# A transformer block in split single precision: more weight pieces in seven products, more low parts by adding transfers

## The chip, the cores and the metric

One core of a Trainium2 chip runs the whole program. The metric is device time in microseconds (us), the median of the runs shown. The kernel before takes 2441.59 us (three runs, 2441.09 to 2441.65).

## The reference, cut to what matters

A block works on 256 tokens of 2048 features in float32: a feed-forward network (FFN), a mixer of two recurrences, cross attention, and a second FFN. The change is in the two FFNs, which have 5632 hidden features:

```python
def swiglu(h, w_up, w_down):
    gate, up = jnp.split(h @ w_up, 2, axis=-1)
    return (jax.nn.silu(gate) * up) @ w_down
...
x = x + 0.5 * swiglu(rms_norm(x, ffn1_norm[l]), ffn1_w_up[l], ffn1_w_down[l])
...
x = x + 0.5 * swiglu(rms_norm(x, ffn2_norm[l]), ffn2_w_up[l], ffn2_w_down[l])
```

`w_up` is 2048 x 11264 and `w_down` 5632 x 2048, so nearly all of an FFN is the streaming of weights through TensorE.

## The kernel before, in words

**Three matmuls for one product.** Every float32 operand is written as a sum of two parts in the type float32r: a high part `h` (the value rounded by ScalarE, line 120) and a low part `l` (value minus `h`, by VectorE, line 121). A product of two such operands is made of three matmuls, high by high, high by low, low by high; `three` (line 446) issues first the pairs that need only the weight's high part (lines 449 and 450), then the ones with its low part (line 452). One matmul here covers 128 x 128 activations by 128 x 512 weights.

**Pieces.** Weights come from DRAM as pieces of 128 x 2048 floats (1 MB). An FFN goes through 11 groups (512 gate columns and 512 up columns) of eight pieces each; piece p holds four blocks of 512 columns (a 2 x 2 arrangement) that meet the activations' pair p. A `plain` piece makes eight products, 24 matmuls. A `fast` piece makes the same contribution with seven products of sums and differences of blocks (the scheme known from Strassen and Winograd), 21 matmuls: VectorE first makes three blocks of differences `td` (lines 213 to 215), and both the three loaded blocks that are still used and the four-block tile of `td` with its copy are split into high and low: `h` and `l` (1536 columns) and `th` and `tl` (2 x 1024 columns, lines 217 to 221). A `mixed` piece makes eight products that add into the same sums as the seven do. `PRODUCTS` (line 458) lists them; in a fast piece the products with `h` and `l` come first (three of them), then the four with `th` and `tl`.

After the groups come `down` pieces (1 MB of `w_down`, 24 matmuls), four after each group from the fourth on, which take up the hidden features of two earlier groups. `turn` (line 483) turns a group's hidden features by transposes on TensorE.

**Order.** `ffn_order` (line 42) writes out the sequence. Before, groups 1 and 2 (counting from 0) have four mixed and four fast pieces; from group 3 on the order is pieces 1, 3, 0, 4, 2, 6, 5, 7 with 0 and 6 mixed. `weights` (line 165) prepares two pieces ahead; the order of instructions on the engines is otherwise set by the framework's scheduler when the program is built. On each engine instructions run in that order, each waiting for its semaphores.

**Low parts by transfers.** The mixed pieces from group 3 on have the kind `added`: `begin_added` (line 186) loads the piece, ScalarE writes `l = -raw`, and a DMA issued by GpSimd (line 192) adds the loaded piece to it, from on-chip memory to on-chip memory; ScalarE then writes `h` into another tile. Since adding into float32r leaves the difference from the rounded value, VectorE has no work on such a piece. `begin_added` is called one piece early.

**Buffers.** Three buffers each of the loaded piece (`raw`), of high parts (`h` and `th` share them), of low parts `l`, and of `wide` (`td`, `tl`, and the sums `ev` at the end of a group). A fast piece takes two of the three `h` buffers, so the `th` of a piece goes where the `h` of the piece before it stood, and can be written only when TensorE is through with that.

**Sums of activations.** A pair that meets fast pieces needs sums and differences of its blocks (`sums` in `operand_pairs`, line 424); a pair that meets mixed pieces needs differences `less` instead. Pairs in `BOTH` (line 403) need both, and keep `less` in an extra slot `xd`.

Of the kernel before, what the change touches and what calls it, by code (L numbers as in the profile page):

```python
# [10 lines left out]
ACT = mybir.ActivationFunctionType  # L11
ALU = mybir.AluOpType
# [7 lines left out]
NG = DFF // 512  # L20
# [21 lines left out]
def ffn_order():  # L42

    out, down = [("plain", 0, p) for p in range(8)], [("down", 0, 1, c, 0) for c in range(4)]
    for g in range(1, NG):
        if g < 3:  # L50
            out += [(("mixed", "fast")[p % 2], g, p) for p in (0, 1, 2, 3, 5, 4, 7, 6)]
        else:
            out += [("mixed" if p in (0, 6) else "fast", g, p) for p in (1, 3, 0, 4, 2, 6, 5, 7)]
        if g > 2 and g % 2:
            down = [("down", g - 2, 2, c, b) for c in range(4) for b in (g - 2, g - 1)]
        n = 2 if g < 3 else 4
        out, down = out + down[:n], down[n:]
    return out + [("down", NG - 2, 2, c, b) for c in range(4) for b in (NG - 2, NG - 1)]
# [3 lines left out]
def block_kernel(ctx: ExitStack, tc: tile.TileContext, xT, xin, memT, vec, gfin, bgate, lruw, wu1, wd1, win, wv,  # L62
                 wg, wab, wout, wq, wk, wvm, wo, wu2, wd2, out_):
    nc = tc.nc
    pe, dve, act, sp = nc.tensor, nc.vector, nc.scalar, nc.sync
# [21 lines left out]
    def slot(dt=F32, name="slot"):  # L87
        return slots.tile([P, 1024], dt, name=name, tag="slot")
# [12 lines left out]
    def col(name, i=0, n=1):  # L101
        a = VEC[name][0] + i
        return vt[:, a:a + n]
# [12 lines left out]
    done = {}  # L116


    def split(h, l, raw):
        done["high"] = act.activation(h, raw, ACT.Copy).ins  # L120
        done["low"] = dve.tensor_tensor(out=l, in0=raw, in1=h.bitcast(F32), op=ALU.subtract).ins  # L121

    def split_tiles():
        return hp.tile([P, 2048], F32R, name="h", tag="h"), lp.tile([P, 2048], F32R, name="l", tag="l")
# [5 lines left out]
    def plan_ffn(name, wu, wd):  # L130
        for e in orders[name]:
            src = wd[e[4], e[3]] if e[0] == "down" else wu[e[1], e[2]]
            kind = "fast" if e[0] == "fast" else "added" if e[0] == "mixed" and e[1] > 2 else "plain"
            plan.append(((name,) + e, src, kind))

    def plan_columns(name, w, which):
# [49 lines left out]
    def begin_added(src):  # L186

        raw = rawp.tile([P, 2048], F32, name="raw", tag="raw")
        l = lp.tile([P, 2048], F32R, name="l", tag="l")
        sp.dma_start(raw, src)  # L190
        act.activation(l, raw, ACT.Copy, scale=-1.0)
        nc.gpsimd.dma_start(l, raw, accum_op=ALU.add)
        return raw, l

    def prepare(src, kind, cuts=1):

        if kind == "added":
            raw, l = begun.pop(0)
            h = hp.tile([P, 2048], F32R, name="h", tag="h")
            done["high"] = act.activation(h, raw, ACT.Copy).ins  # L200
            return h, l
        raw = rawp.tile([P, 2048], F32, name="raw", tag="raw")
        n = 2048 // cuts
        if kind == "plain":
            h, l = split_tiles()
            for a in range(0, 2048, n):
                sp.dma_start(raw[:, a:a + n], src[:, a:a + n])
                split(h[:, a:a + n], l[:, a:a + n], raw[:, a:a + n])
            return h, l
        sp.dma_start(raw, src)  # L210
        td = scoped["wide"].tile([P, 2048], F32, name="td", tag="wide")
        two = [v[:, a:a + 1024].rearrange("p (i n) -> p i n", i=2) for v, a in ((td, 0), (raw, 512))]
        dve.tensor_tensor(out=two[0], in0=raw[:, None, :512].broadcast_to([P, 2, 512]), in1=two[1], op=ALU.subtract)
        dve.tensor_tensor(out=td[:, 1024:1536], in0=raw[:, 1024:1536], in1=td[:, :512], op=ALU.subtract)
        dve.tensor_tensor(out=td[:, 1536:], in0=raw[:, 1536:], in1=td[:, 1024:1536], op=ALU.subtract)
        h, l = split_tiles()
        split(h[:, 512:], l[:, 512:], raw[:, 512:])
        th = hp.tile([P, 2048], F32R, name="h", tag="h")
        tl = scoped["wide"].tile([P, 2048], F32R, name="tl", tag="wide")
        for a in (0, 1024):  # L220
            split(th[:, a:a + 1024], tl[:, a:a + 1024], td[:, a:a + 1024])
        return (h, l), (th, tl)
# [177 lines left out]

    BOTH = [2, 4]
    xd = []

    def operand_pairs(src, gain, q, xg, out):

        for a in src:
            i = len(out)
            g = xg[:, i * 512:(i + 1) * 512]  # L410
            for z in range(2):
                act.activation(g[:, z * T:][:, :T], a[:, z * T:(z + 1) * T], ACT.Copy,
                               scale=col(gain, 4 * q + 2 * i + z))
            h, l = slot(F32R, "xh"), slot(F32R, "xl")
            split(h[:, :512], l[:, :512], g)
            less = None if i else (h[:, 512:768], l[:, 512:768])
            if 2 * q + i in BOTH:
                if 2 * q + i == BOTH[0]:
                    xd.append(slot(F32R, "xd"))
                n = 512 * BOTH.index(2 * q + i)  # L420
                less = [xd[-1][:, a:a + 256] for a in (n, n + 256)]
            out.append(((h, l), less))

        def sums(which=((0, "less"), (0, "sums"), (1, "less"), (1, "sums"))):
            s = slot(name="xs")
            for i, ((h, l), less) in enumerate(out):
                a = [xg[:, i * 512 + j * P:][:, :P] for j in range(4)]

                def made(h, l, n, at, terms):
                    o = [s[:, at + j * P:][:, :P] for j in range(n)]  # L430
                    for j, (x, y, op) in enumerate(terms(o)):
                        dve.tensor_tensor(out=o[j], in0=x, in1=y, op=op)
                    split(h, l, s[:, at:at + n * P])

                if less and (i, "less") in which:
                    made(*less, 2, 0, lambda o: ((a[0], a[1], ALU.subtract), (a[2], a[3], ALU.subtract)))
                if (i or 2 * q in BOTH) and (i, "sums") in which:
                    if not i and len(which) > 1:
                        s = slot(name="xs")
                    made(h[:, 512:], l[:, 512:], 4, 512 * i,  # L440
                         lambda o: ((a[1], a[3], ALU.add), (o[0], a[0], ALU.subtract),
                                    (a[1], a[0], ALU.subtract), (a[2], o[1], ALU.subtract)))

        return sums
# [154 lines left out]
    def late_sums(q):  # L599
        with tc.issue_after(done["low"]):  # L600
            sums1[q](((0, "sums"),))

    for q, i in ((1, 16), (2, 17)):
        rest[i] = lambda q=q: late_sums(q)


# [580 lines left out]
```

## Time and profile before

| | |
|---|---|
| median of three runs | 2441.59 us |
| the profiled execution, its own time | 2441.09 us |
| its span, first to last instruction | 2439.3 us |
| outside the span | 1.8 us |
| first FFN, roughly | 0 to 670 us |
| second FFN, roughly | 1770 to 2430 us |
| one group from group 4 on (eight pieces and four down pieces) | 62.1 us |
| adding transfers | 32 |

The profile is one execution. PE is TensorE, DVE VectorE, ACT ScalarE, POOL GpSimd, SP the engine that issues the loads. A group of instructions is told by its line, its engine, its operation and `output<-inputs`. A matmul's own time (0.39 us) is longer than the distance between two starts, since they overlap; time on TensorE is therefore read from starts. The view in order of time has start, duration, engine, line, operation and, in brackets, idle time ahead of it with what ended it.

### The profile page before, as it was taken

The page shows a single profiled execution, that of the slowest core. Times are in us where ns is not written, and L with a number is a line of the kernel's source. Part 1 is how long each engine was busy: PE and PEld are TensorE (multiplying, and loading weights), DVE is VectorE, ACT ScalarE, POOL GpSimd, SP SyncE. Part 2 cuts the span into 40 slices and gives each one's busy share as a digit, 9 for nine tenths or more (in the row PEclk, how much of TensorE's full clock was granted, in tenths as well). Part 3 has the DMA queues.
Part 4 walks back from the last instruction along what each step waited for, and adds up shares of the span by engine and source line. Part 5 has one row for each costly group of instructions (what it writes and reads, how often), then busy time and mean ns, then how long its engine had stood idle before and what let it go on. Part 6 is the DMA issues. An engine that isn't in the chain of part 4 may idle for free.

```text
span 2439.3 us, 30196 instructions
## 1 busy us (share of the span) xinstructions
PE 2428.9 (100%) x12250; PEld 2034.0 (83%) x12250; DVE 1889.8 (77%) x2015; ACT 1394.5 (57%) x1399; POOL 28.1 (1%) x36
## 2 busy tenths in 40 slices
PE   9999999999999999999999999999999999999998
PEld 8888888888888888888888888888888888888887
DVE  7999999999865767577565676556589999999995
ACT  8566666666554454477435554455555666666664
POOL 0000000000000000000000000000000000000000
PEclk9999999999999999999999999999999999999999
DMA  7577767777655445445555555444555777777774
GB/s 293 194 224 258 250 233 236 234 238 237 214 188 190 173 173 182 173 172 216 194 186 190 209 192 188 172 172 156 190 190 187 249 238 233 234 238 242 237 234 150
DMA packets 75308, 509.69 MB, mean 209 GB/s; under 512 B 8352, under 2 KB 8608, under 8 KB 15264
## 3 DMA queue, kind: packets, MB, share of 16 engines
q1 hardware_dynamic: 69840, 473.06, 53.9%
q0 software_dynamic: 4608, 33.56, 6.8%
q8 instruction: 96, 1.57, 0.3%
q10 hardware_dynamic: 720, 1.13, 0.1%
q14 instruction: 44, 0.36, 0.0%
HBM read 472.07 MB, written 2.10 MB: 194 GB/s over the span
## 4 chain that ended last, share of the span: by engine, by line
PE 98%; DVE 1%; DMA 0%; ACT 0%; issue 0%; ACTq 0%; SPq 0%; DVEq 0%
PE acc L449 18%; PE acc L450 18%; PE acc L452 18%; PE acc L231 11%; PE acc L252 8%; PE acc L253 8%; PE acc L255 8%; PE acc L235 6%; PE acc L488 1%; PE acc L389 1%; DMA raw<-wu 0%; PE acc L764 0%; PE acc L1046 0%; PE acc L1001 0%; PE acc L867 0%; PE warm L109 0%
## 5 line engine op out<-in xcount | busy, mean ns | idle before, releaser
L121 DVE TENSOR_TENSOR l<-raw,h 128x2048 fp32r<-128x2048 f32 (+2 forms) x420 | 872.8, 2085 | 357.9 <-ACT h L120 346.1
L120 ACT ACTIVATE h<-raw 128x2048 fp32r<-128x2048 f32 (+2 forms) x420 | 732.8, 1752 | 626.2 <-PE acc L253 204.5
L449 PE MATMUL acc<-h,xh 128*128 128x512 f32 x1280 | 498.3, 390 | 0.4 <-ACT h L120 0.4
L450 PE MATMUL acc<-h,xl 128*128 128x512 f32 x1280 | 496.9, 389 | 0.0
L120 ACT ACTIVATE h<-td 128x1024 fp32r<-128x1024 f32 x224 | 229.2, 1055 | 180.1 <-PE acc L450 137.5
L252 PE MATMUL acc<-h,ops 128*128 128x512 f32 x832 | 326.9, 393 | 0.0
L253 PE MATMUL acc<-h,ops 128*128 128x512 f32 x832 | 324.3, 390 | 0.0
L121 DVE TENSOR_TENSOR tl<-td,h 128x1024 fp32r<-128x1024 f32 x224 | 267.0, 1220 | 32.3 <-ACT h L120 29.9
L449 PEld LDWEIGHTS acc<-h,xh 128*128 128x128 f32 x1280 | 240.3, 188 | 51.1 <-ACT h L120 1.1
L450 PEld LDWEIGHTS acc<-h,xl 128*128 128x128 f32 x1280 | 240.3, 188 | 49.5
L231 PE MATMUL acc<-ops,h 128*128 128x512 f32 x1152 | 278.0, 393 | 0.3
L449 PE MATMUL acc<-h,hidop 128*128 128x512 f32 x704 | 275.8, 392 | 0.0
L450 PE MATMUL acc<-h,hidop 128*128 128x512 f32 x704 | 274.3, 390 | 0.0
L231 PEld LDWEIGHTS acc<-ops,h 128*128 128x128 f32 x1152 | 211.9, 188 | 42.9 <-DVE ops L292 0.9
L452 PE MATMUL acc<-l,xh 128*128 128x512 f32 x832 | 218.6, 389 | 0.0
L255 PE MATMUL acc<-l,ops 128*128 128x512 f32 x832 | 206.1, 390 | 0.0
L452 PE MATMUL acc<-l,hidop 128*128 128x512 f32 x704 | 188.3, 389 | 0.0
L255 PEld LDWEIGHTS acc<-l,ops 128*128 128x128 f32 x832 | 156.2, 188 | 32.4
L252 PEld LDWEIGHTS acc<-h,ops 128*128 128x128 f32 x832 | 156.2, 188 | 32.3
L452 PEld LDWEIGHTS acc<-l,xh 128*128 128x128 f32 x832 | 156.1, 188 | 32.4
L253 PEld LDWEIGHTS acc<-h,ops 128*128 128x128 f32 x832 | 156.3, 188 | 31.6
L452 PEld LDWEIGHTS acc<-l,hidop 128*128 128x128 f32 x704 | 132.1, 188 | 27.5
(218 smaller groups left out, 2355.0 us busy)
## 6 DMA issues: line engine op xcount, KB each, us to landing
raw<-wu SPq DMA_DIRECT2D x172, 1024.0 KB, 4.9
raw<-wd SPq DMA_DIRECT2D x88, 1024.0 KB, 4.8
raw<-win SPq DMA_DIRECT2D x40, 1024.0 KB, 4.8
l<-raw POOLq DMA_DIRECT2D x32, 1024.0 KB, 7.3
raw<-wg SPq DMA_DIRECT2D x32, 1024.0 KB, 4.8
raw<-wab SPq DMA_DIRECT2D x16, 1024.0 KB, 4.8
raw<-wout SPq DMA_DIRECT2D x16, 1024.0 KB, 4.8
raw<-wq SPq DMA_DIRECT2D x16, 1024.0 KB, 4.8
```

The source lines that it names most:

```text
L120: done["high"] = act.activation(h, raw, ACT.Copy).ins
L121: done["low"] = dve.tensor_tensor(out=l, in0=raw, in1=h.bitcast(F32), op=ALU.subtract).ins
L231: pe.matmul(acc, h[:, k * P:(k + 1) * P], xs[k], start=k == 0, stop=False)
L235: done["product"] = pe.matmul(acc[:, :T], l[:, k * P:(k + 1) * P], xs[k][:, :T], start=False, stop=k == KT - 1).ins
L252: pe.matmul(accs[t], x[:, t * P:][:, :P], h[j], start=first and j == 0, stop=False)
L253: pe.matmul(accs[t], x[:, T + t * P:][:, :P], h[j], start=False, stop=False)
L255: done["product"] = pe.matmul(accs[t], x[:, t * P:][:, :P], l[j], start=False, stop=last and j == 3).ins
L389: pe.transpose(accs[m // 2][:, m % 2 * T + t * P:][:, :P], tile[:, t * 512 + m * P:][:, :P], ident)
L449: pe.matmul(acc, ah, bh, start=start, stop=False)
L450: pe.matmul(acc, al, bh, start=False, stop=False)
L452: pe.matmul(acc, ah, bl, start=False, stop=stop)
L488: pe.transpose(acc[:, z * T + t * P:][:, :P], hid[t][:, (2 * y + z) * P:][:, :P], ident)
```

## The change

From group 3 on the order becomes 1, 3, 4, 0, 2, 5, 6, 7 with only piece 0 mixed, so seven of eight pieces are fast. The kinds change with it. Mixed pieces become plain to prepare (VectorE makes their low part). Pieces 3, 4, 5 and 6 become `fast added`: as fast, but the low part of their three loaded blocks is made by ScalarE (`-raw`) and an adding transfer of 1536 columns. Down pieces of blocks 2, 4, 6 and 8 with an odd column c become `added` (8 per FFN). All adding transfers now read the piece from DRAM a second time, not the loaded tile. Pair 6 now needs both kinds of sums, which adds a second `xd` slot and one more late piece of sums in the first FFN.

```diff
         if g < 3:
             out += [(("mixed", "fast")[p % 2], g, p) for p in (0, 1, 2, 3, 5, 4, 7, 6)]
         else:
-            out += [("mixed" if p in (0, 6) else "fast", g, p) for p in (1, 3, 0, 4, 2, 6, 5, 7)]
+            out += [("fast" if p else "mixed", g, p) for p in (1, 3, 4, 0, 2, 5, 6, 7)]
...
-            kind = "fast" if e[0] == "fast" else "added" if e[0] == "mixed" and e[1] > 2 else "plain"
+            kind = "fast" if e[0] == "fast" else "plain"
+            if e[0] == "down" and 0 < e[4] < NG - 1 and e[4] % 2 == 0 and e[3] % 2:
+                kind = "added"
+            if e[0] == "fast" and e[1] > 2 and e[2] in (3, 4, 5, 6):
+                kind = "fast added"
...
-        nc.gpsimd.dma_start(l, raw, accum_op=ALU.add)
+        nc.gpsimd.dma_start(l, src, accum_op=ALU.add)
...
         h, l = split_tiles()
-        split(h[:, 512:], l[:, 512:], raw[:, 512:])
+        if kind == "fast":
+            split(h[:, 512:], l[:, 512:], raw[:, 512:])
+        else:
+            act.activation(l[:, 512:], raw[:, 512:], ACT.Copy, scale=-1.0)
+            nc.gpsimd.dma_start(l[:, 512:], src[:, 512:], accum_op=ALU.add)
+            done["high"] = act.activation(h[:, 512:], raw[:, 512:], ACT.Copy).ins
...
-    BOTH = [2, 4]
+    BOTH = [2, 4, 6]
...
-                if 2 * q + i == BOTH[0]:
+                n = 512 * (BOTH.index(2 * q + i) % 2)
+                if not n:
                     xd.append(slot(F32R, "xd"))
-                n = 512 * BOTH.index(2 * q + i)
...
-    for q, i in ((1, 16), (2, 17)):
+    for q, i in ((1, 16), (2, 17), (3, 18)):
         rest[i] = lambda q=q: late_sums(q)
```

## The prediction

> **What bounds the kernel now.** I read the page first (span, busy shares, chain that ended last), then what TensorE waited for, then one group of an FFN in order of time.
>
> ```profile
> span 2439.3 us, 30196 instructions
> PE 2428.9 (100%) x12250; PEld 2034.0 (83%) x12250; DVE 1889.8 (77%) x2015; ACT 1394.5 (57%) x1399; POOL 28.1 (1%) x36
> PE 98%; DVE 1%; DMA 0%; ACT 0%; issue 0%; ACTq 0%; SPq 0%; DVEq 0%
> PE acc L449 <- ACT h L120: 0.4, 1, 0.4
> ```
>
> The chain is 98% TensorE, and after the warm-up its only wait for another engine is 0.4 us. Nothing but fewer matmuls can shorten this, and there is no wait to remove. A busy PE could still be a slow one, so the stages and starts come next: one group in the windows view (columns: PE, PEld, DVE, ACT, POOL busy, granted clock, DMA share, GB/s), then starts on TensorE in one group.
>
> ```profile
> 400.00:462.10 62.10, 62.10 (x281) 51.51 (x279) 57.34 (x56) 38.37 (x32) 1.73 (x2) 1.00 0.73 237
> 100.00:160.00 60.00, 60.00 (x270) 49.57 (x269) 58.69 (x60) 32.56 (x27) 1.00 (x1) 1.00 0.61 211
> 1790.00:1850.00 60.00, 60.00 (x268) 49.31 (x268) 56.92 (x54) 32.16 (x26) 0.00 (x0) 1.00 0.57 200
> ```
>
> ```profile
> 368.29 0.39 PE L449 MATMUL acc<-h,xh 128*128 128x512 f32 x1
> ...
> 371.69 0.39 PE L450 MATMUL acc<-h,xl 128*128 128x512 f32 x1
> 371.91 1.98 PE L452 MATMUL acc<-l,xh 128*128 128x512 f32 x8
> 373.73 0.39 PE L449 MATMUL acc<-h,xh 128*128 128x512 f32 x1
> ...
> 378.49 0.39 PE L449 MATMUL acc<-h,xh 128*128 128x512 f32 x1
> ...
> 382.34 1.07 PE L452 MATMUL acc<-tl,xh 128*128 128x512 f32 x4
> 383.25 0.39 PE L449 MATMUL acc<-h,hidop 128*128 128x512 f32 x1
> ```
>
> The clock is full (1.00). Piece 6, mixed, runs from 368.29 to 373.73: 24 matmuls in 5.44 us, 0.2267 us each. Pieces 5 and 7, fast, take 4.76 us each, 21 times the same. VectorE is second: 57.34 of a group's 62.10 us, 4.8 us idle.
>
> **What the change removes.** Piece 6 of groups 3 to 10 becomes fast in both FFNs: 16 pieces lose 3 matmuls. In the order in which the programs' instructions stand, TensorE has 48 fewer, 16 each of lines 449, 450 and 452 of before. 48 x 0.2267 = 10.88 us. All of it lies on the chain. A group shrinks by 0.68 us to 61.42.
>
> **What it adds to the other engines, per group.** These rows of VectorE and ScalarE give prices (distances between starts, since neighbours overlap by 0.08 us).
>
> ```profile
> 330.55 2.28 DVE L121 TENSOR_TENSOR l<-raw,h 128x2048 fp32r<-128x2048 f32 x1
> 332.75 0.68 DVE L558 SCALAR_TENSOR_TENSOR x<-acc,x 128x512 f32<-128x512 f32 x1
> ...
> 349.15 1.22 DVE L213 TENSOR_TENSOR td<-raw 128x1024 f32<-128x1024 f32 x1
> 350.40 0.69 DVE L214 TENSOR_TENSOR td<-raw,td 128x512 f32<-128x512 f32 x1
> 351.13 0.69 DVE L215 TENSOR_TENSOR td<-raw,td 128x512 f32<-128x512 f32 x1
> 351.74 1.75 DVE L121 TENSOR_TENSOR l<-raw,h 128x1536 fp32r<-128x1536 f32 x1
> 353.41 2.35 DVE L121 TENSOR_TENSOR tl<-td,h 128x1024 fp32r<-128x1024 f32 x2
> 355.68 1.22 DVE L213 TENSOR_TENSOR td<-raw 128x1024 f32<-128x1024 f32 x1
> ...
> 376.43 2.36 DVE L121 TENSOR_TENSOR tl<-td,h 128x1024 fp32r<-128x1024 f32 x2 [0.98 <-ACT h L120]
> ```
>
> ```profile
> 372.16 1.49 ACT L120 ACTIVATE h<-raw 128x1536 fp32r<-128x1536 f32 x1 [3.20 <-PE acc L450]
> 375.33 2.01 ACT L120 ACTIVATE h<-td 128x1024 fp32r<-128x1024 f32 x2 [1.68 <-PE acc L450]
> 377.25 1.90 ACT L120 ACTIVATE h<-raw 128x2048 fp32r<-128x2048 f32 x1
> ```
>
> VectorE: one more set of `td` (1.25 + 0.73 + 0.61) and `tl` (2.27), 4.86; three fewer `l` of 1536 columns (six fast before, three of seven after), 3 x 1.67 = 5.01; one `l` of 2048 less for a down piece and one more for piece 0, 2.2 each. Sum -0.15 us: as busy as before, in a shorter group. ScalarE: six sets of `h` and `th` (1.4 + 1.9 each), two operations of 1.8 for each of two mixed pieces and one for each down piece made 34.2; seven sets, four negated copies of 1536 (1.4 each), one of 1.8 for piece 0, four for the down pieces and one negated copy make 39.5: 5.3 more on top of the 38.4 that the window shows, 44 of 61.4. Both engines have room on average; what matters is when.
>
> **The step that decides: piece 7.** Before, VectorE had no work in the two mixed pieces, a rest of two times 5.44 us. Its second half of piece 7's `tl` ended at 376.43 + 2.36 = 378.79, and TensorE wanted it two matmuls after 382.34: 4.0 us of lead. After, pieces 5 and 6 cost VectorE 2.59 + 2.27 = 4.86 us against TensorE's 4.76 and piece 7 costs 6.53, so the lead goes. I work it out from the last point where VectorE must wait for TensorE: `th` of piece 5 goes into the buffer of piece 2's `h`, free after the first 6 matmuls of piece 2. Above, ScalarE starts 0.25 us after a release (371.91 to 372.16); a negated copy just ahead of it costs 0.04 more. From the release:
> - 0.29, then 1.06 for half of `th`, 0.05 to VectorE: 1.40.
> - VectorE in the changed order: `tl` of 5 (2.27), `td` of 6 (2.59), 0.1 waiting for the second half of `th`, `tl` of 6 (2.27), first `td` of 7 (1.14), its `l` (1.67), second `td` (0.61), first half of `tl` (1.14), third `td` (0.61), then the `l` of the first down piece (2.20), which stands ahead of the second half of `tl` (1.22): 15.82. Done at 17.22.
> - TensorE wants it after the rest of piece 2 (15 matmuls), pieces 5 and 6 (42) and 19 of piece 7: 76 x 0.2267 = 17.23.
>
> The lead is 0.01 us: nil. Bounds of the stall: nothing, if any step is a little shorter; 1.1 us a group, if the 14 operations take full durations instead of overlapping by 0.08. The rows show overlap nearly throughout, so I take 0.1 us, 16 times: 1.6 us. Behind the waiting matmul stands the whole of TensorE, so a stall here is paid in full.
>
> **The transfers.** A new wait: `l` of pieces 3 to 6 needs copy, issue and landing.
>
> ```profile
> L192 POOL DMA_DIRECT2D l<-raw x32: 859/865/1002, 153.9 to 2337.2; - x32
> ...
> DMA to landing us min/median/max: 7.1/7.3/13.2
> ```
>
> ```profile
> raw<-wu SPq DMA_DIRECT2D x172, 1024.0 KB, 4.9
> ...
> q1 hardware_dynamic: 69840, 473.06, 53.9%
> q0 software_dynamic: 4608, 33.56, 6.8%
> ```
>
> The tightest is piece 4: its `l` takes the buffer of the last down piece, free as piece 1 begins; the copy stands behind an `h`, so 0.8 + 1.5 us later the transfer is issued, and TensorE wants it 9.52 + 14 x 0.2267 = 12.69 us in. It may take 10.3 us; piece 6 may take 10.7. No row shows an adding transfer from DRAM. Bounds: a plain load of 1 MB, 4.9; the slowest adding one, 13.2. I take under 7.3 (three quarters of the bytes): covered with 3 us to spare, so nothing. Load on the queues: by the shares, 1 MB costs 2.9 us of 16 engines as a load (0.539 x 2439 / 451 MB) and 5.2 us adding (0.068 x 2439 / 32); a group goes from 12 loads and 2 to 12 and an equivalent of 4, 56 of 61.4 us, 0.91 where the window says 0.73. Loads then land later: one that meets an adding transfer of 1536 columns (3.9) needs up to 8.8, and the same schedule issues loads 8 to 11 us ahead of their first use: nothing, or a part of a microsecond on an engine that still has a lead there.
>
> One rule speaks against five GpSimd transfers a group. VectorE's operations nearly all read two on-chip tiles, and the issue took 859 to 1002 ns throughout, beside a VectorE that was busy 57 of 62 us. The Trainium skill (SBUF — State Buffer, SBUF: two separate sides) says that VectorE's two-port operations lock GpSimd out of a shared port, so that its descriptors are late: 3.1 us where 0.62 was the time alone. By that, 2.5 us more would leave piece 4 a lead of 0.5 us, still no loss by itself. The narrow spread of the issues does not bear it out here.
>
> **The sums for pair 6.** Once in each FFN: four operations of 128 columns and one split.
>
> ```profile
> L432 DVE TENSOR_TENSOR xs<-xg 128x128 f32<-128x128 f32 x40 | 9.7, 282 | 0.0
> L121 DVE TENSOR_TENSOR xl<-xg,xh 128x512 fp32r<-128x512 f32 x16 | 11.0, 690 | 11.7 <-ACT xh L120 11.3
> ```
>
> 4 x 0.28 + 0.69 = 1.8 us of VectorE. In the first FFN they stand near 103 us, where VectorE has 1.31 us idle in 60: at least 0.5 and at most 1.8 shows on TensorE; I take 1.2. In the second FFN 3.1 us are idle: nothing, at most 1.8.
>
> **Sum.** Against the profiled execution's 2441.09 (2439.3 and 1.8 around it): - 10.88 + 1.6 + 1.2 = 2433.0. The median of the runs is 0.5 above: 2433.5 us.
>
> **The rivals.**
> 1. No stall at all: TensorE stays gapless and 48 matmuls go: 2430.7. For it: the leads of 3 to 4 us before; against: piece 7's is used up by the schedule above.
> 2. VectorE becomes the bound at piece 7, slower than before. With a stall s per group the time is 2431.9 + 16 s. For it: the schedule leaves nothing, and VectorE has 98% of its time taken at 100 to 160 us already. Against: 1.1 us needs every overlap lost. At s = 0.5 it gives 2439.9 (within 0.2% of before), at s = 1.1 2449.5; it decides from s = 0.6.
> 3. Low parts land late. With landing L a group loses (L - 10.3) + (L - 10.7): from 10.8 the gain is gone. At 13.2, the largest shown, 5.4 x 16 = 86 us: about 2520. For it: 0.91 of the engines taken, a DRAM source that no row shows. Against: 7.3 in all but a few.
>
> **How the numbers follow.** Small stalls as summed 0.52, with own range 2431 to 2437; none at all 0.19; VectorE's stall between 0.3 and 0.9 a group, within 0.2% of before, 0.13; over that 0.09; late landings 0.07. 0.2% is 4.9 us, about what a measurement of this kernel tells from no change. So faster 0.71, same 0.13, slower 0.16. The range goes from 2430, just under rival 1, to 2442, which takes in most of the middle case and leaves out slower ones.
>
> **What would show it.** In the changed profile: 48 fewer matmuls; starts of fast pieces 4.76 us apart, groups 61.4 to 61.6. A wait of TensorE on line 121's `tl` once a group, at piece 7, is the decisive step; a wait on `l` with the landing over 10 us is rival 3, a wait on ScalarE's `th` would mean that the negated copies stand in the way, which I count at nothing. The landing of the 1536-column transfers should read 5 to 7.3, DMA share about 0.9. The prediction is wrong if TensorE waits over 0.3 us in most groups, or if gaps at 100 to 160 us pass 2 us.

## The result, and the profile after

The changed kernel takes 2456.68 us (median of four runs, 2455.61 to 2457.71) against 2441.34 before: ratio 1.0063, 95% interval 1.0049 to 1.0077. It is slower by 15 us where 8 us less were forecast, and outside the range. Rival 3, low parts that land late, is what happened. Times below are medians; one of the ten runs of `load_later` took 3304.75 us at a granted clock of 0.686 and is left out of its median.

The page of the changed kernel, its span, busy shares and the chain that ended last:

```profile
span 2455.6 us, 30385 instructions
PE 2427.0 (99%) x12202; PEld 2025.3 (82%) x12202; DVE 1883.5 (77%) x2057; ACT 1486.4 (61%) x1481; POOL 70.1 (3%) x84
PE 88%; DMA 9%; ACT 1%; DVE 1%; issue 1%; ACTq 0%; SPq 0%; DVEq 0%
```

The 48 matmuls are gone (12250 to 12202) and VectorE's and ScalarE's shares are near what was worked out. New is 9% of the chain on DMA. What TensorE and its weight loads waited for (total us, times, longest):

```profile
PE acc L461 <- DMA l<-wu: 17.7, 19, 2.7
PE acc L458 <- ACT h L120: 0.8, 1, 0.8
...
PEld acc L461 <- DMA l<-wu: 26.7, 23, 3.2
PEld acc L461 <- DVE tl L121: 0.3, 1, 0.3
```

Nearly every wait is the first low-part matmul of a piece waiting for an adding transfer; VectorE's `tl`, the step called decisive, made 0.3 us. Read from the starts of matmuls in both FFNs, what the distances have over 0.2267 us adds up to 4.6 us before and 31.0 after, 23.7 of it at line 461 on `l`. 31.0 - 4.6 - 10.9 (the matmuls that went) = 15.5, against 2455.6 - 2439.3 = 16.3 in the spans: nearly the whole loss is stalls. Of the 23.7 us 15.4 stand at piece 6, fifteen stalls, one a group: in the last seven groups of the first FFN, and in all eight groups with transfers of the second. 3.8 more stand at pieces 5 and 6 of the first FFN's first group with transfers, the fourth group (group 3 in the code).

The adding transfers of the fast pieces, and the page's issues (median us to landing) and queues:

```profile
L225 POOL DMA_DIRECT2D l<-wu x64: 865/874/1007, 152.5 to 2362.8; - x64
...
DMA to landing us min/median/max: 6.8/9.7/12.8
```

```profile
q1 hardware_dynamic: 69840, 473.06, 52.5%
q0 software_dynamic: 11520, 67.11, 14.7%
...
raw<-wu SPq DMA_DIRECT2D x172, 1024.0 KB, 6.1
...
l<-wu POOLq DMA_DIRECT2D x64, 768.0 KB, 9.7
```

Three quarters of the bytes take 9.7 us where 1 MB took 7.3. Loads take 6.1 where they took 4.9. The issue on GpSimd stayed at 865 to 1007 ns.

One group (columns as in the prediction), then the end of piece 6 in the group before it, in order of time on TensorE:

```profile
411.60:473.20 61.60, 61.60 (x277) 50.82 (x276) 56.50 (x58) 44.26 (x36) 4.36 (x5) 1.00 0.91 270
```

```profile
383.77 0.39 PE L459 MATMUL acc<-h,xl 128*128 128x512 f32 x1
384.84 0.97 PE L461 MATMUL acc<-l,xh 128*128 128x512 f32 x3 [0.68 <-DMA l<-wu]
385.65 1.09 PE L461 MATMUL acc<-tl,xh 128*128 128x512 f32 x4
```

The group is as forecast (61.6 us, VectorE 56.5, ScalarE 44, DMA 0.91). Piece 6's low part was due at 384.0 and came 0.68 us later. Its transfer and the load next to it, by the rows of SP and POOL:

```profile
373.09 0.33 SPq L211 DMA_DIRECT2D raw<-wd  x1
...
373.40 0.89 POOL L225 DMA_DIRECT2D l<-wu  x1 [4.87 <-DVE td L219]
...
DMA to landing us min/median/max: 11.4/11.4/11.4
```

11.4 us from issue to landing, with 10.7 allowed by the prediction: 0.7 over, and the wait is 0.68 (0.84 by the starts). The allowance was nearly right; the landing wasn't. The same rows in the kernel before, for a piece 6 of its first FFN and a piece 6 at the start of the second:

```profile
415.61 0.33 SPq L210 DMA_DIRECT2D raw<-wu  x1
...
418.30 0.86 POOL L192 DMA_DIRECT2D l<-raw  x1 [15.26 <-ACT l L191]
...
DMA to landing us min/median/max: 7.2/7.2/7.2
...
1902.98 0.33 SPq L210 DMA_DIRECT2D raw<-wu  x1
...
1903.02 0.86 POOL L192 DMA_DIRECT2D l<-raw  x1 [16.65 <-ACT l L191]
...
DMA to landing us min/median/max: 13.2/13.2/13.2
```

Here a cause suggests itself, before any change: with a load issued 2.7 us ahead the transfer took 7.2 us, with one issued 0.04 us ahead 13.2. All three of the old kernel's 32 transfers with a load 0.7 us or less ahead took 11.0 to 13.2 us. After the change piece 6's transfer has a load about 0.3 us ahead of it in nearly every group (0.31 in the one shown). That is read off afterwards; the runs below had to show it.

### The profile page after: what moved, and what is told of

Same layout as the page of the kernel before. It is cut to its first block, busy times and chain, and to the rows that moved or that the text cites. A ratio compares the mean times of both kernels' runs of the same rounds, so it can differ in the third digit from the quotient of the medians.

```text
span 2455.6 us, 30385 instructions
## 1 busy us (share of the span) xinstructions
PE 2427.0 (99%) x12202; PEld 2025.3 (82%) x12202; DVE 1883.5 (77%) x2057; ACT 1486.4 (61%) x1481; POOL 70.1 (3%) x84
## 4 chain that ended last, share of the span: by engine, by line
PE 88%; DMA 9%; ACT 1%; DVE 1%; issue 1%; ACTq 0%; SPq 0%; DVEq 0%
PE acc L461 16%; PE acc L458 14%; PE acc L459 14%; PE acc L240 11%; DMA l<-wu 8%; PE acc L261 8%; PE acc L262 8%; PE acc L264 8%; PE acc L244 5%; ACT l L224 1%; PE acc L497 1%; DMA raw<-wu 1%; PE acc L398 1%; ACT h L120 0%; PE acc L773 0%
## 5 line engine op out<-in xcount | busy, mean ns | idle before, releaser
L121 DVE TENSOR_TENSOR l<-raw,h 128x2048 fp32r<-128x2048 f32 (+2 forms) x372 | 790.0, 2128 | 337.0 <-ACT h L120 335.4
L120 ACT ACTIVATE h<-raw 128x2048 fp32r<-128x2048 f32 (+2 forms) x372 | 662.0, 1784 | 471.3 <-PE acc L262 205.7
L458 PE MATMUL acc<-h,xh 128*128 128x512 f32 x1256 | 490.6, 391 | 0.8 <-ACT h L120 0.8
L459 PE MATMUL acc<-h,xl 128*128 128x512 f32 x1256 | 488.9, 390 | 0.0
L120 ACT ACTIVATE h<-td 128x1024 fp32r<-128x1024 f32 x256 | 266.0, 1057 | 180.2 <-PE acc L459 88.8
L121 DVE TENSOR_TENSOR tl<-td,h 128x1024 fp32r<-128x1024 f32 x256 | 308.5, 1221 | 68.5 <-ACT h L120 66.9
L461 PE MATMUL acc<-l,xh 128*128 128x512 f32 x744 | 202.6, 394 | 17.7 <-DMA l<-wu 17.7
L461 PEld LDWEIGHTS acc<-l,xh 128*128 128x128 f32 x744 | 138.2, 188 | 54.1 <-DMA l<-wu 26.7
L217 DVE TENSOR_TENSOR td<-raw 128x1024 f32<-128x1024 f32 x128 | 155.9, 1218 | 6.1 <-DMA raw<-wu 3.9
## 6 DMA issues: line engine op xcount, KB each, us to landing
l<-wd POOLq DMA_DIRECT2D x16, 1024.0 KB, 10.7
```

What stands on the lines that cost most here:

```text
L458: pe.matmul(acc, ah, bh, start=start, stop=False)
L459: pe.matmul(acc, al, bh, start=False, stop=False)
L461: pe.matmul(acc, ah, bl, start=False, stop=stop)
```

## The experiments

Ratios are to the kernel before, run beside it on the same chip, with a 95% interval. The theories: Q, two transfers issued close together hold each other up; S, the source in DRAM makes them slow; L (or D), the load on the DMA engines as a whole does; T, TensorE loses what the time to land exceeds the time allowed by; V, VectorE is late instead; and, later, N and H, what was issued just ahead of a transfer sets its landing (G: it doesn't). A first or last record is that of the transfer itself in the trace of DMA records, in us after its issue.

**Order of the pieces (spread).** The pieces with transfers are no longer neighbours.

```diff
-(1, 3, 4, 0, 2, 5, 6, 7)]
+(1, 3, 2, 4, 0, 5, 7, 6)]
```

> Only the order of the pieces of a group from group 3 on is changed, to 1, 3, 2, 4, 0, 5, 7, 6: the four pieces with adding transfers (3, 4, 5, 6) no longer come two in a row, and their number and bytes are the same. Theory Q (the changed kernel lost because two adding transfers and the loads between them come faster than the 16 DMA engines move them, so the second of two lands late): landing of the 768 KB transfers falls from a median of 9.7 us to about 8 or less, TensorE's waits on them from 44 us to under 10, time 2431 to 2438. Theory S (an adding transfer that reads DRAM is slow in itself): landing stays at 9 to 10 us and the time over 2445. Theory L (the load as a whole, 0.9 of the engines, is too much): landing stays over 9 us, waits on it spread over all four pieces, time over 2445.

2486.73 us, ratio 1.0187 [1.0172, 1.0202]. The waits of TensorE:

```profile
PE acc L458 <- ACT h L120: 20.6, 16, 2.4
PE acc L461 <- DMA l<-wu: 15.5, 14, 4.8
```

As the whole cause theory Q falls: the waits on `l` are nearly as long with the pairs apart, and waits on ScalarE's `h` come on top. Piece 4, now without a transfer or a load close by, has its first record at 1.6 us and lands in about 7. Pieces 5 and 6, with a load 0.7 to 2.1 us ahead or 0.24 us behind, still have first records at 2.6 to 4.9 us.

**The source (tile_source).** The transfers add the loaded tile, as before, not DRAM.

```diff
-            nc.gpsimd.dma_start(l[:, 512:], src[:, 512:], accum_op=ALU.add)
+            nc.gpsimd.dma_start(l[:, 512:], raw[:, 512:], accum_op=ALU.add)
```

(and the same in `begin_added`.)

> The changed kernel with every adding transfer reading the loaded tile on the chip, as before the change, in place of DRAM; the loaded tile is then held until the transfer has landed. Theory S: landing of the 768 KB transfers falls to 7 us or less, TensorE's waits on them go, time 2431 to 2438. Theory Q: the engines move the same bytes, so landing stays at 9 to 10 us and the loads come later as well: time 2450 to 2475.

2468.68 us, 1.0114 [1.0099, 1.0130].

```profile
l<-raw POOLq DMA_DIRECT2D x64, 768.0 KB, 8.1
```

```profile
PE acc L461 <- DMA l<-raw: 11.9, 9, 4.9
PE acc L458 <- ACT h L120: 11.3, 12, 2.2
```

The landing falls by 1.6 us and a third of the wait with it, but the tile is kept longer, loads come later, and waits on `h` take the place. The DRAM source is the better of the two, and a DMA record takes the same time from either (see the end): S is at most a part of the cause.

**Fewer transfers (one_of_pair, no_adding).** Fast pieces 3 and 5 only, then none at all (nor for down pieces).

```diff
-            if e[0] == "fast" and e[1] > 2 and e[2] in (3, 4, 5, 6):
+            if e[0] == "fast" and e[1] > 2 and e[2] in (3, 5):
```

> The changed kernel with adding transfers for pieces 3 and 5 alone; the low parts of 4 and 6 go back to VectorE. Theory Q: landing falls to 7 to 8 us and TensorE does not wait for it; VectorE has 3.3 us more in a group, about 60.5 of 61.4, and its lead at piece 7 is gone: 0.5 to 2 us a group on line 121's tiles, time 2440 to 2465. Theory S: half of the waits on the transfers remain, at both pieces that keep them.

> The changed kernel without any adding transfer: every low part by VectorE. 8.9 us more a group on VectorE, about 66 us of work for 61.4: VectorE becomes the bound, at 4.6 us or more a group, time 2505 to 2530 by every theory. If it is much less, the transfers were not needed.

one_of_pair 2449.71 us, 1.0037 [1.0023, 1.0051]; no_adding 2488.21 us, 1.0193 [1.0172, 1.0213]. Window 400 to 600 us, in that order:

```profile
400.00:600.00 200.00, 199.60 (x890) 162.99 (x889) 190.59 (x191) 132.30 (x111) 8.71 (x10) 1.00 0.80 245
```

```profile
400.00:600.00 200.00, 195.92 (x847) 154.23 (x846) 197.86 (x192) 114.10 (x96) 0.00 (x0) 1.00 0.55 198
```

Without transfers VectorE is the bound (197.86 of 200), so they are needed; no_adding cost less than expected. With two a group the landing was still 9.3 us, though the next adding transfer was at least 14 us away: theory Q expected 7 to 8. VectorE took two pieces more, and yet the kernel is 7.0 us faster than the changed one.

**Time to land against time allowed (tl_first, own_low, own_tl).** Three kernels give the late pieces more time: `tl`'s matmuls first; a fourth buffer for the `l` of pieces 4 and 6; both.

```diff
-        for acc, (ah, al), (bh, bl), _, stop in products:
+        n = 3 if len(products) == 7 else 0
+        for acc, (ah, al), (bh, bl), _, stop in products[n:] + products[:n]:
```

```diff
+        if kind == "fast own":
+            l = Later(scoped["low"].tile([P, 1536], F32R, name="l", tag="low"))
+        else:
+            l = lp.tile([P, 2048], F32R, name="l", tag="l")
```

> The changed kernel with one edit: a fast piece's seven low-part matmuls begin with the four on tl, and the three on l come last (piece order, transfers and loads stay). Theory T (each adding transfer lands as it does, 9 to 12 us after its issue, and the loss is only what it exceeds its time by): pieces 3, 4 and 6 get 4 x 0.2267 = 0.91 us more, piece 5 none, since its l buffer also comes free that much later. The stalls of the changed kernel in the first half (1.31, 1.08, 0.84, 0.07, 1.35, 1.14, 2.26 us at piece 6) shrink by 0.9 each, the stalls on l from 23.7 us to about 9, the time to 2440 to 2446; landing of the 768 KB transfers stays at 9 to 10 us in the median. Rival D (the DMA engines' load is what limits, and a stall only gives it time): the time stays above 2452 and waits on h or on l come back later in each group. Rival V (the late low part of tl was as near): waits of L461 on DVE tl of over 5 us appear.

> The changed kernel with a fourth buffer for low parts: pieces 4 and 6 of the groups from the fourth on keep their l in a tile of 1536 columns of its own, so that the negation of piece 6 needn't wait for piece 0's product. (For room, the scratch tile of the squares is bfloat16 in the ffn stages, and one ring of the small pool has two buffers, not three.) In the changed kernel that negation began at 371.50 us behind piece 0's product, while piece 6's raw tile was there by 369.35 us, so the transfer can be issued about 2 us earlier. Theory T: the stalls of 0.4 to 1.4 us at piece 6 go, 2436 to 2443 us. Rival A (an earlier issue only stands longer behind the transfer of piece 5 and the loads): first packets 5 to 6 us after the issue in place of 4, landing 11 to 13 us, and the time stays above 2450. Rival D (load as a whole): above 2452, with waits on h.

> Both edits at once: the four low matmuls on tl first, and the fourth buffer for the low parts of pieces 4 and 6. Theory T: no stall on l is left outside group 3; the time is that of before less most of the 10.88 us of the removed matmuls, 2431 to 2437. Rival D: within 3 us of the better of the two single edits or above 2445.

tl_first 2448.38 us, 1.0031 [1.0020, 1.0042]; own_low 2471.53, 1.0128 [1.0111, 1.0146]; own_tl 2473.71, 1.0135 [1.0117, 1.0153].

With `tl` first the landing stays at 9.8 us and the stalls on `l`, read from starts, fall from 23.7 to 10.2 us. That bears out T: what is lost is what the landing exceeds the allowance by. The time ended 2 us above the range expected. The fourth buffer failed for a reason not foreseen. ScalarE's negation of piece 6 then, in order of time:

```profile
377.82 1.49 ACT L235 ACTIVATE l<-raw 128x1536 fp32r<-128x1536 f32 x1 [0.58 <-DMA raw<-wu]
```

It no longer waits for a buffer but for its own load, which came late: in this group the transfer's issue is 6.9 us behind piece 5's, not 5.7, and the stalls at piece 6 are 1.2 to 3.3 us. None of the rivals named before says this. The median landing, 11.1 us, is in the range of rival A. Piece 4 shows one thing more. In most groups its transfer now goes out 1.4 us behind piece 3's with next to no load records between (3 at most). Its first record comes at 4.6 to 5.0 us, when piece 3's transfer is nearly through, and it lands in 11.9 to 13.4 us where it took 8.9 to 10.6. An adding transfer just ahead holds the next one up too, so theory Q is a part of the truth.

**Own size (half_low).** The transfers bring 1024 columns, VectorE subtracts 512.

```diff
-            act.activation(l[:, 512:], raw[:, 512:], ACT.Copy, scale=-1.0)
-            nc.gpsimd.dma_start(l[:, 512:], src[:, 512:], accum_op=ALU.add)
+            act.activation(l[:, 1024:], raw[:, 1024:], ACT.Copy, scale=-1.0)
+            nc.gpsimd.dma_start(l[:, 1024:], src[:, 1024:], accum_op=ALU.add)
+            split(h[:, 512:], l[:, 512:], raw[:, 512:])
...
```

The old line that makes all of `h` goes.

> The changed kernel, but the adding transfers of fast pieces bring only the last 1024 of the 1536 columns (512 KB, packets of 4096 B); VectorE subtracts the other 512 (about 0.68 us more a piece, 2.7 a group, where it has 4 to 5 us left of 62.6). It tells own size from what lies ahead: if the landing is mainly the transfer's own packets, it falls by a third, from 9.7 to about 6.5 us, and the waits on DMA l go, 2435 to 2445 us; if it is mainly what stands ahead of its first packet (4 us) and loads among its packets, landing falls by 1.7 us at the most (a third of the 5 us of its own), to 8 or more, and the time comes to 2440 to 2450. Either way VectorE's share in the window 400 to 600 us rises from 0.93 or so towards 0.97; if waits on DVE l or tl of over 10 us appear, VectorE has become the bound.

2526.60 us, 1.0348 [1.0332, 1.0365].

```profile
PE acc L458 <- ACT h L120: 28.2, 25, 4.1
PE acc L461 <- DVE tl L121: 9.7, 13, 2.6
PE acc L461 <- DVE l L121: 6.8, 4, 4.5
```

No wait on a transfer is left and the landing is 6.5 us, but with 0.68 us more of VectorE ahead of each `tl` the waits move to `h`, `tl` and `l` made by the engines. The run says little of the landing, since stalls space the transfers out; it says how little lead VectorE has.

**The DMA engines' load (down_plain).** The down pieces' transfers, 18 to 20 us away from the others, go.

```diff
-                kind = "added"
+                kind = "plain"
```

> The changed kernel without the adding transfers of the down pieces (one down piece in four): VectorE makes those 16 low parts again, 2.29 us each, one a group. The transfer that goes was issued at 393.66 us, 20 us after piece 6's (373.39) and 18 us before the next piece 3's (411.76). Theory N (what lies just ahead in the queues sets the landing): the first packets stay at +1.6 us for pieces 3 and at +4 us or more for the others, the median landing stays between 9.3 and 10, and piece 6 waits as before; the waits of the low weight loads on DMA l stay at 20 to 27 us. Theory L (the DMA engines' share of the whole stage sets it): the share in 400 to 600 us falls from 0.90 to about 0.85 and the landing with it to 8.5 to 9, the waits to half. Time by N 2454 to 2465 (VectorE's 2.29 us a group cost little or some), by L 2445 to 2452.

2459.77 us, 1.0074 [1.0059, 1.0089]. The window, and the waits:

```profile
400.00:600.00 200.00, 198.29 (x887) 163.26 (x886) 187.14 (x186) 133.39 (x111) 10.45 (x12) 1.00 0.78 247
```

```profile
PE acc L461 <- DMA l<-wu: 17.9, 20, 3.2
```

DMA share 0.90 to 0.78, landing 9.8 (piece 6's last record at 10.97 us, 11.04 in the changed kernel), waits 17.9 against 17.7: the share of the stage isn't the cause, and N holds but for a detail. In most groups piece 3's first record came at 4.6 to 4.9 us and not at 1.6, where a load now went out 0.14 us behind its issue: a load just behind gets ahead as well.

**Transfers elsewhere (three_tl, early, early_fa).** With `tl` first: no transfer for piece 6; transfers for piece 0 and two down pieces in four, begun a piece early, and for no fast piece; for piece 0, pieces 3 and 4 and one down piece in four. The first edit is three_tl's; the second is in early and early_fa, which also limit the fast pieces and the down pieces as said.

```diff
-            if e[0] == "fast" and e[1] > 2 and e[2] in (3, 4, 5, 6):
+            if e[0] == "fast" and e[1] > 2 and e[2] in (3, 4, 5):
```

```diff
-            kind = "fast" if e[0] == "fast" else "plain"
+            kind = "fast" if e[0] == "fast" else "added" if e[0] == "mixed" and e[1] > 2 else "plain"
```

> The kernel with tl's low matmuls first, and no adding transfer for piece 6 (VectorE subtracts its 1536 columns again, 1.75 us a group). In the kernel with tl first the stalls left on l over 0.3 us are 8, seven of them at piece 6 or in the fourth group, 8.1 us together. Theory N: with that transfer out, piece 5's is the last of its group and lands in 9 to 10.5 us, no stall on l over 0.5 us is left after the fourth group, and the time is 2436 to 2444. Theory L agrees in the sign but expects landing of all of them to fall by the share (0.90 to 0.85). Rival V: VectorE at 0.94 of the stage makes pieces late and the time stays at 2447 to 2453, with waits on ScalarE's h and DVE's tl in place of DMA l.

> The seven products of the changed kernel with tl's low matmuls first, but the adding transfers where the kernel before had its kind: piece 0 whole, its load, negation and transfer begun a piece ahead, and two of the four down pieces, begun a piece ahead as well; no fast piece has one. So 3 MB of adding transfers a group against 2 before and 4 in the changed kernel. Theory T (time to land decides): landing of the 1 MB transfers 9 to 11 us, none late, waits on DMA l under 3 us; VectorE does all 1536-column low parts of the fast pieces, 7 us a group more than in the changed kernel less 4.6, so it stands at about 0.95 of the stage; 2432 to 2442 if that is enough, over 2445 with waits on h and tl if it isn't (rival V, as where only pieces 3 and 5 had transfers, 2449.7).

> Tl's low matmuls first; adding transfers for piece 0 whole (begun a piece ahead), for fast pieces 3 and 4, and for one down piece in four: 3.5 MB a group. Pieces 5 and 6, where the changed kernel waited, have VectorE's low parts. Piece 0's load and transfer now stand between piece 3's and piece 4's, so piece 4 has what piece 6 had: theory N expects first packets of +4 us or more and late low parts there, 2440 to 2450; theory L (share about 0.87) 2440 or less, with no place that waits above the others. VectorE's share is 0.92 to 0.94.

three_tl 2460.64 us, 1.0079 [1.0064, 1.0094]; early 2580.69, 1.0572 [1.0556, 1.0587]; early_fa 2588.43, 1.0601 [1.0584, 1.0619]. One row each, in that order:

```profile
PE acc L462 <- DVE tl L121: 11.8, 7, 3.9
```

```profile
PE acc L462 <- DMA l<-wd: 99.6, 18, 7.4
```

```profile
PE acc L462 <- DMA l<-wu: 104.2, 16, 9.1
```

In three_tl piece 6's 1.75 us put back on VectorE cost more than its late transfer (rival V). The other two were far worse than expected, and T's small waits for early were wrong: in the transfer records most of its transfers stand 0.4 to 1.8 us behind a load and the down pieces' land 11.6 us after issue, and in early_fa piece 4's stands behind piece 0's, 4.7 us ahead, and among loads, with first records at +4.3 to +7.3 us and last ones at +11 to +16.

**What stands ahead.** Read record by record, medians of the groups after the first with transfers, first FFN (us after the issue; a 1 MB load has 128 records; the last column counts records of loads that start while the transfer's own run):

```
kernel, piece        first record   last record   load records among
before, 0                1.63           6.97              1
before, 6                1.49           6.98             15
changed, 3               1.59           6.70             27
changed, 4               3.98           8.92             44
changed, 5               3.69           9.16             89
changed, 6               4.14          11.04            165
one_of_pair, 5           4.64           9.41             43
own_low, 4               4.83          11.77            137
```

Piece 3's transfer, with the last load ahead issued 5.7 us before it in most groups, is as fast as those before. Two things can stand ahead of a transfer. One is a load: in one_of_pair one goes out within 0.05 us of piece 5's transfer, and 117 to 129 records of loads run between that issue and the transfer's first record, in both FFNs. Piece 4 of the changed kernel, with its load 1.7 us ahead, has 115 to 128 in most groups. The other is an adding transfer still under way, as in own_low at piece 4. Piece 6 of the changed kernel has both: piece 5's transfer, whose last record comes 3.2 to 4.8 us after piece 6's issue, and the load 0.31 us ahead, whose records run partly ahead of piece 6's own (133 load records in the group shown, 24 to 58 in nine others) and partly among them. load_later moves this one load, the first down piece's: a write of one column, queued on ScalarE behind piece 6's `h`, keeps it back.

```diff
+            if e[0] == "down" and plan[-1][0][1:2] == ("fast",) and plan[-1][0][2] > 2:
+                kind = "plain later"
...
+        if kind == "plain later":
+            with tc.issue_after(done["six"]):
+                act.activation(raw[:, :1], ones[:, :1], ACT.Copy)
+            kind = "plain"
...
-            done["high"] = act.activation(h[:, 512:], raw[:, 512:], ACT.Copy).ins
+            done["high"] = done["six"] = act.activation(h[:, 512:], raw[:, 512:], ACT.Copy).ins
```

> The changed kernel with one load moved: the load of the first down piece of a group, which SP issued 0.30 us before piece 6's adding transfer (373.09 against 373.39 us), waits for a write of one column by ScalarE behind piece 6's h, so that it goes out some 3 us after the transfer. Theory H (a transfer's first packet waits for the packets of a load issued in the 2 us before it; with the load 2.4 us or more ahead, as in the kernel before, or none, the first packet comes at +1.5): first packets of piece 6's transfers at +1.5 to +2.5 us in place of +4.0 to +4.4, its landing 7 to 9.5 us, and its 15 stalls, 15.4 us together, go: 2440 to 2446 us. The down piece's load comes 3.3 us later and lands at about 382, its h was made at 384.25; if that is too tight, waits on ScalarE's h of 2 us or less a group appear. Rival G (the packets of the adding transfer are slow themselves or stand behind what all queues hold): first packets stay at +4 and more, the stalls stay, 2455 to 2470.

2444.66 us, 1.0016 [1.0007, 1.0026]: 12.0 us of the 15.3 come back with one load a group issued 3.3 us later. SP, POOL and landing of the same group, then window and waits:

```profile
371.66 0.89 POOL L231 DMA_DIRECT2D l<-wu  x1 [4.58 <-DVE td L225]
...
374.68 0.33 SPq L217 DMA_DIRECT2D raw<-wd  x1
...
DMA to landing us min/median/max: 9.1/9.1/9.1
```

```profile
400.00:600.00 200.00, 200.00 (x899) 165.50 (x899) 181.07 (x186) 141.67 (x122) 14.80 (x17) 1.00 0.90 273
```

```profile
PE acc L467 <- DMA l<-wu: 4.7, 4, 2.8
```

Landing 11.4 to 9.1, TensorE busy throughout in 400 to 600 us at the same DMA share of 0.90, and of the fifteen stalls at piece 6 one of 0.25 us is left. Instead `tl` of piece 7 is now late once a group, by 0.06 to 0.36 us, 2.4 us in all. One detail was wrong: first records come at 3.60 us, not 1.5 to 2.5, since piece 5's transfer is still ahead (its last record at +4.05 in this group). So most of the gain isn't at the start of the transfer: the load's records come after the transfer's and no longer among them (last record 11.04 to 8.11, load records among 165 to 44).

**What is left (load_later_tl, load_later_g4, later_g3_34, later_g3_345, later_g4).** On top of the load moved: `tl` first; that and no transfers for fast pieces in the fourth group; and, with `tl` in its old place, no transfers in that group for pieces 5 and 6, for piece 6, or for all four.

```diff
-            if e[0] == "fast" and e[1] > 2 and e[2] in (3, 4, 5, 6):
+            if e[0] == "fast" and e[1] > 2 and e[2] in (3, 4, 5, 6) and (e[1] > 3 or e[2] < 5):
```

(later_g3_34; `e[2] < 6` in later_g3_345, `e[1] > 3` alone in the two g4.)

> The load moved and tl's low matmuls first, both: by theory H with 0.91 us more for pieces 3, 4 and 6 what is left of waits on DMA l is the fourth group's (2 us) and piece 4's, under 4 us in all; 2434 to 2442 us. Rival G: as with tl's low matmuls first alone, 2447 to 2455.

> As the last, and fast pieces have adding transfers only from the fifth group on: the fourth group, where stalls of 0.88 and 2.90 us stood in the changed kernel in the first half, has VectorE's low parts. By theory H with the low parts' place in the start of the transfers: 1 to 4 us less than the last, 2432 to 2440. Rival V: VectorE's 7 us more in that one group make it late in both halves, and the time is 2 to 8 us over the last.

> The kernel with the load moved (tl's matmuls in their first place), and in the fourth group, the first with adding transfers, only pieces 3 and 4 have them. With the load moved, stalls of 0.68 and 3.00 us were left at pieces 5 and 6 of that group (186.91 and 193.91 us). Theory H with the start of the transfers as its last weak place: these go and VectorE's 3.5 us are covered: 2440 to 2443 us, no faster than before. Rival V: VectorE falls behind and the waits move to tl or h, 2445 to 2452 us.

> As the last, but only piece 6 of the fourth group is without an adding transfer: VectorE has 1.75 us more there. The stall of 3.00 us goes and the 0.68 may stay: 2440.5 to 2443.5 us by theory H, 2445 to 2450 by rival V.

> As the load moved, and adding transfers of fast pieces only from the fifth group on. With tl's matmuls first this gave 2458.8 us, with waits on DVE tl of 17 us. If it was tl's earlier place that made these, the time comes to 2440 to 2447 here; if it was VectorE's 7 us more in the fourth group, it stays above 2450.

In this order: 2450.32 us, 1.0039 [1.0024, 1.0054]; 2458.77, 1.0071 [1.0055, 1.0088]; 2452.62, 1.0049 [1.0036, 1.0063]; 2449.99, 1.0034 [1.0021, 1.0047]; 2454.21, 1.0055 [1.0043, 1.0068]. A row of TensorE's waits in load_later_tl:

```profile
PE acc L468 <- DVE tl L121: 5.8, 8, 3.1
```

All go to rival V. load_later_tl came into the range given to rival G, but not for G's reason: its stalls on `l` are 4.0 us, against 10.2 with `tl` first alone, and `tl` itself is late, with waits on `h` besides. One, two or four pieces of one group given back to VectorE (1.75, 3.5, 7 us in each FFN) cost 5.3, 8.0 and 9.6 us over load_later, and a stall of 3.1 us on `tl` appears in the next group (load_later_tl has one of 3.3 us at that place and gives no piece back). So the stall of 3.00 us that load_later keeps in the fourth group can't be bought off this way. No kernel tried beats the one before.

## Why the prediction was wrong

**What held.** The removal: 48 matmuls, and in load_later groups of 61.5 us, with no stall over 0.1 us from 400 to 600 us. The loads on engines and queues. The issue on GpSimd: at 865 to 1007 ns beside a VectorE busy 56.5 of 61.6 us, the 2.5 us priced for late descriptors didn't show. The allowances, nearly: the prediction has 10.3 us for piece 4 (its own terms, 12.69 less 0.8 and 1.5, give 10.4) and 10.7 for piece 6, and by the stalls these had 10.0 to 10.1 and 10.6. Piece 7's `tl`, 1.6 us forecast: in the changed kernel its wait hides behind piece 6's (0.3 us in the profile), and with the load moved it comes out, once a group, 2.4 us in all. That VectorE has no lead there was right, also by the runs that gave it more: 0.68 us more in each of four pieces cost 70 us. The sums for pair 6, 1.2 us in the forecast, hardly show: from 100 to 160 us the stalls are 0.3 us after and 0.2 before. A stall of 1.0 us on `h` at 173.6 us has no cause shown.

**What failed** is one term: "I take under 7.3 (three quarters of the bytes): covered with 3 us to spare, so nothing." It was priced by the median of the transfers before and by bytes. Measured: 9.7 in the median, and 10.6 to 12.8 at the fifteen pieces 6 that made 15.4 of the 23.7 us of stalls on `l`. The bounds, 4.9 to 13.2, held it; the choice between them was made without asking what set the 13.2. The row of 1903.02 points to it: a load had gone out 0.04 us earlier. The new order has a load released about 0.3 us ahead of piece 6's transfer in nearly every group, with piece 5's transfer still under way, and the prediction, which counted DMA as a share, never placed loads and transfers in one order of time. Moving that load alone brought 12.0 of the 15.3 us back. Rival 3 had the late landing, its threshold ("from 10.8 the gain is gone") and 7% of the chance; what it gave as grounds, a high share of the engines and the DRAM source, is not what decides: down_plain had 0.78 and the same landing, and with the tile as the source the kernel was 12 us slower still.

**What would have shown it.** The landing's spread before (7.1/7.3/13.2) split by the time to the last load ahead, then the releases in the changed order. The Trainium skill (DMA: Bandwidth & Descriptors, Queues, rings and completion order) says that a DMA engine takes turns between queues by packets of some 9 to 17 descriptors. A load is 128 records on 16 engines, 8 on each if they are spread evenly, so by that rule it passes in one turn; the trace of one_of_pair agrees, with 117 to 129 load records ahead of the first of piece 5's transfer.

**Still open.** Of the stalls on `l` 8.3 us stood elsewhere, 3.8 of them in the fourth group of the first FFN, and load_later keeps 3.7 of those; whether a load or a transfer ahead makes them too wasn't tried. Nor was it tried how much of piece 6's landing is due to piece 5's transfer. That loads slowed from 4.9 to 6.1 us didn't show as waits in the changed kernel, but own_low met it.

## What to carry to other kernels

Price a transfer by its neighbours, not by bytes or the queues' average share: here these were loads issued in the 2 us before it or within 0.3 us behind it, and adding transfers still under way. Put loads and transfers of the new order on one time line, and split the spread of landings in the old profile by that. Where a transfer has a deadline and a load next to it has slack, issue the load some microseconds behind it. And where the second engine has no lead, look first for remedies that leave its work alone: of the runs that bought time to land with VectorE's time, only one_of_pair gained on the kernel it changed, and none got below the kernel before.

## What the hardware showed beside this

After a stall TensorE ran slow. Windows of the changed kernel (granted clock is the next to last but one number) around two waits, of 2.74 us up to 193.78 and of 2.09 up to 636.46, and after one of 1.15 us up to 259.79:

```profile
188.00:193.00 5.00, 3.04 (x14) 2.18 (x12) 3.05 (x3) 1.92 (x3) 0.00 (x0) 1.00 1.03 296
194.00:198.00 4.00, 4.00 (x12) 3.19 (x13) 4.00 (x5) 1.54 (x2) 0.00 (x0) 0.66 0.66 274
630.00:636.00 6.00, 4.37 (x20) 3.28 (x18) 6.00 (x7) 4.24 (x4) 0.00 (x0) 1.00 1.00 317
637.00:641.00 4.00, 4.00 (x12) 3.12 (x11) 3.00 (x2) 0.75 (x1) 0.00 (x0) 0.57 0.77 287
...
259.80:263.80 4.00, 4.00 (x18) 3.31 (x19) 3.31 (x3) 3.42 (x3) 0.00 (x0) 1.00 0.56 174
```

The granted clock is 0.66 and 0.57 in the 4 us after the two longer ones and 1.00 after the short one. At 0.66 and 0.57, 4 us do the work of 2.6 and 2.3, so each of these two waits cost another 1.4 to 1.7 us by estimate. The length of a wait alone doesn't decide: load_later has one of 2.84 us up to 193.92, and its clock stays full:

```profile
194.00:198.00 4.00, 4.00 (x18) 3.30 (x19) 4.00 (x5) 2.58 (x2) 0.00 (x0) 1.00 0.72 301
```

The Trainium skill (TensorE: Matmul & The Clock Gate, Part 1: The HAM clock gate) lets the clock fall after an idle window of about 3.4 us; here pauses of 2.74 and 2.09 us were enough, and one of 2.84 us was not.

An adding record of 8192 B took 0.63 us in the median, from DRAM (the changed kernel) or from the tile (the kernel before), and a load's 0.31: byte for byte an adding transfer holds the engines twice as long as a load, so one adding transfer is itself much for the next to stand behind.
